# The first two rows of x as two half transfers on two queues, and four stores for six

## The chip, the cores and the metric

The kernel runs on one core of a Trainium2 chip. The metric is the time of one execution on the device in microseconds, and the median of several runs is what is compared. The profile comes from one execution of its own.

## The reference

```python
def reference(x, y):                      # x, y: 8 x 4096 x 512, float32
    gram = np.matmul(x, y.transpose(0, 2, 1))
    diag = np.diagonal(gram, axis1=1, axis2=2)
    diag = diag - diag.max(axis=-1, keepdims=True)
    exp = np.exp(diag)
    return (exp / exp.sum(axis=-1, keepdims=True)).astype(np.float32)
```

Only the diagonal of the product is used. So the work is 8 x 4096 dot products of 512 elements each, and a softmax over the 4096 results of each of the 8 batches. Both inputs have 67 MB, and every byte is read once. The output has 0.13 MB.

## The kernel before

**Tiling.** Four batches form a set, so there are two sets. A set lies on 128 partitions as 4 batches by 32 groups, and each partition holds 128 consecutive rows (of 512 floats) of one batch. A step `t` takes 32 of these rows on each partition: 64 KB of x and 64 KB of y per partition, 8.4 MB each. There are four steps for each set, eight steps in all (`S`). x has two buffers, `xs[0]` and `xs[1]`, used in turn; y has one, `ys`. The tile `side` holds a copy of the last 6 rows of y (`K`), so that the buffer of y comes free sooner.

**The first six steps** (the loop over `range(S - 2)`). `load_x` and `load_y` each issue one transfer of 128 partitions by 64 KB on SyncE's queue. ScalarE copies the last six rows of y to `side`. VectorE multiplies x by y in place: `products` with 26 rows of `ys`, then with the 6 rows of `side` (L78). It then sums 30 of the 32 rows (`sums`, L81), and ScalarE sums the other two (`sums_act`, L86). The order within an engine is written out by hand. SyncE issues its transfers in the program's order, each once its buffer is free and an earlier transfer that used the same completion counter has landed. There are eight such counters, taken in turn.

**The last two steps.** Step 6 loads in one piece and leaves most sums to ScalarE. Step 7 loads x and y in pieces that become smaller towards the end, and VectorE does the dot products row by row (L89) as the pieces land. The last piece is 320 columns of the last row of x (L185).

**The ends.** At the start ScalarE loads the table for the exponential (L124), VectorE and ScalarE each execute an alignment instruction, VectorE writes one constant, and SyncE executes two drains (L130, L131) and then issues the first x. After step 3 the first set's maxima and exponentials are made, and its result `res[0]` is complete in step 4. It is stored only at the end, behind all loads on SyncE's queue, in six pieces of 16, 16, 16, 16, 32 and 32 partitions (L192). The second set's softmax follows the last dot product (`exps`, `normalize`), and ScalarE issues the store of `res[1]` (L194).

Of the kernel before, what the change touches and what calls it, by code (L numbers as in the profile page):

```python
# [11 lines left out]
def kernel(  # L12
# [6 lines left out]
    nc = tc.nc  # L19
# [6 lines left out]
    P = nc.NUM_PARTITIONS  # L26
# [3 lines left out]
    R = 32  # L30
    H = R // 2
# [3 lines left out]
    L = 9  # L35
    E = 64
    V = 5 * D // 8
    U = D - V
    S = B // Q * (C // R)


    xv = x.rearrange("(s b) (j c) d -> s (b j) c d", b=Q, j=G)
# [10 lines left out]
    xs = [t[:, : R * D].rearrange("p (r d) -> p r d", d=D) for t in xflat]  # L53
# [6 lines left out]
    def columns(t, r0, n):  # L60
        c0 = t % (C // R) * R + r0
        return slice(c0, c0 + n)

    def rows(t, r0, n):
        return xs[t % 2][:, r0 : r0 + n, :]

    def dots_of(t, r0, n):
        return diag[t * R // C][:, columns(t, r0, n)]

    def load_x(t, r0, n):  # L70
        nc.sync.dma_start(out=rows(t, r0, n), in_=xv[t * R // C, :, columns(t, r0, n), :])  # L71

    def load_y(t, r0, n):
        nc.sync.dma_start(out=ys[:, r0 : r0 + n, :], in_=yv[t * R // C, :, columns(t, r0, n), :])  # L74

    def products(t, r0, n, yt):
        xt = rows(t, r0, n)
        nc.vector.tensor_tensor(out=xt, in0=xt, in1=yt, op=Alu.mult)  # L78

    def sums(t, r0, n):  # L80
        nc.vector.tensor_reduce(out=dots_of(t, r0, n), in_=rows(t, r0, n), axis=X, op=Alu.add)  # L81

    def sums_act(t, r0, n):
        for r in range(r0, r0 + n):
            row = xs[t % 2][:, r, :]
            nc.scalar.activation(out=row, in_=row, func=Act.Copy, accum_out=dots_of(t, r, 1))  # L86

    def dot(xt, yt, out):
        nc.vector.scalar_tensor_tensor(  # L89
            out=xt, in0=xt, scalar=1.0, in1=yt, op0=Alu.mult, op1=Alu.mult, accum_out=out  # L90
        )

    def dots(t, r0, n):
        for r in range(r0, r0 + n):
            dot(xs[t % 2][:, r, :], ys[:, r, :], dots_of(t, r, 1))
# [12 lines left out]
    def exps(i, d):  # L108
        mxp = small.tile([P, 1], f32, name=f"mxp{i}")
        largest(mxp, d)  # L110
        nmx = over_quadrant(f"nmx{i}", mxp, Alu.max, negate=True)
        sump = small.tile([P, 1], f32, name=f"sump{i}")
        nc.scalar.activation(out=res[i], in_=diag[i][:, :C], func=Act.Exp, bias=nmx, scale=1.0, accum_out=sump)  # L113
        return sump

    def normalize(i, sump):
        total = over_quadrant(f"sum{i}", sump, Alu.add)
        rc = small.tile([P, 1], f32, name=f"rc{i}")
        nc.vector.reciprocal(out=rc, in_=total)  # L119
        nc.vector.tensor_single_scalar(out=res[i], in_=res[i], scalar=rc, op=Alu.mult)  # L120
# [10 lines left out]
    nc.sync.drain()  # L131

    for t in range(S - 2):
        load_x(t, 0, R)
        load_y(t, 0, R)
        nc.scalar.activation(out=side, in_=ys[:, R - K :, :], func=Act.Copy)  # L136
        if t == C // R:
            normalize(0, sump)
        products(t, 0, R - K, ys[:, : R - K, :])
        products(t, R - K, K, side)  # L140
        sums(t, 0, R - W)
        sums_act(t, R - W, W)
        if t == C // R - 1:
            sump = exps(0, diag[0])

    t = S - 2
# [13 lines left out]
    chained = xflat[t % 2][:, R * D : R * D + 1]  # L160
    late = R * D - V
    upto = {load_x: 0, load_y: 0}
# [15 lines left out]
    end = ((t % (C // R)) + 1) * R * D  # L178
    nc.sync.dma_start(out=xt[:, first : late], in_=xrow[:, end - R * D + first : end - V])
    dots(t, done, 1)  # L180
    load_y(t, R - 2, 1)
    dots(t, R - 2, 1)
    load_y(t, R - 1, 1)
    dot(xt[:, late - U : late], yflat[:, late - U : late], chained)
    nc.sync.dma_start(out=xt[:, late : R * D], in_=xrow[:, end - V : end])  # L185
    dot(xt[:, late : R * D + 1], yflat[:, late : R * D + 1], dots_of(t, R - 1, 1))
# [1 line left out]
    met = small.tile([P, C - R], f32, name="met")  # L188
    nc.scalar.activation(out=met, in_=diag[1][:, : C - R], func=Act.Copy)  # L189

    for p, n in ((0, H), (H, H), (2 * H, H), (3 * H, H), (4 * H, 2 * H), (6 * H, 2 * H)):
        nc.sync.dma_start(out=ov[0, p : p + n, :], in_=res[0][p : p + n, :])  # L192
    normalize(1, exps(1, diag[1][:, C - R + H :]))
    nc.scalar.dma_start(out=ov[1], in_=res[1])  # L194
# [30 lines left out]
```

## Time and profile before

| What | us |
|---|---|
| timed runs: median (lowest, highest) | 320.44 (320.05, 320.58), 3 runs |
| profiled execution: span from the first to the last instruction | 318.4 |
| median of the runs less that span | 2.04 |
| VectorE busy | 241.7, in 101 instructions |
| ScalarE busy | 49.8, in 97 instructions |
| DMA, mean over the span | 422 GB/s |

The profile gives the span of its execution but not that execution's whole time, so the runs' median stands beside it. In the parts that follow, "L78" is line 78 of the kernel before. "SPq" and "ACTq" are the queues on which SyncE and ScalarE issue transfers; the time on such a line is that of the issue, not of the transfer. A piece "DMA ys" in the chain is the time from the issue of a load of y to its landing. In a windows line the columns are the window, its length, the busy time of VectorE (DVE), ScalarE (ACT) and GpSimd (POOL) with the number of instructions, the granted clock, the mean busy share of the 16 DMA engines, and GB/s. A DMA packet is counted in the window in which it starts, so in a short window the share can be over 1.

### The profile page before, as it was taken

How to read it: one execution, taken by the hardware profiler on the slowest of the kernel's cores; microseconds unless marked ns; L12 is line 12 of the kernel's file. 1: busy time of each engine (PE TensorE's matmuls, PEld its weight loads, DVE VectorE, ACT ScalarE, POOL GpSimd, SP SyncE). 2: the span in 40 equal slices, each digit the busy share in tenths (PEclk: the TensorE clock that was granted, in tenths of full speed). 3: DMA queues.
4: the chain of work that ended last, by engine and by line, in shares of the span. 5: the costliest groups of instructions: out<-in, count | busy, mean ns of one | idle time of the engine just before them, and what ended most of it. 6: DMA issues, size and time to landing. Idle time of an engine off the chain costs nothing.

```text
span 318.4 us, 320 instructions
## 1 busy us (share of the span) xinstructions
DVE 241.7 (76%) x101; ACT 49.8 (16%) x97; POOL 0.2 (0%) x4
## 2 busy tenths in 40 slices
DVE  0000079994899939999399994999939998499995
ACT  1000030100301003010020102101030100496700
POOL 0000000000000000000000000000000000000000
DMA  9999999999999999999999999999999999999993
GB/s 397 395 395 510 412 395 453 469 395 395 486 436 395 453 469 395 395 486 436 395 395 519 403 395 461 461 395 395 527 395 395 486 436 395 425 415 432 434 410 140
DMA packets 3970, 134.37 MB, mean 422 GB/s; under 512 B 512, under 2 KB 896, under 8 KB 1536
## 3 DMA queue, kind: packets, MB, share of 16 engines
q1 hardware_dynamic: 3824, 134.29, 97.9%
q10 hardware_dynamic: 144, 0.07, 0.1%
q14 instruction: 2, 0.02, 0.0%
HBM read 134.22 MB, written 0.13 MB: 422 GB/s over the span
## 4 chain that ended last, share of the span: by engine, by line
DMA 70%; DVE 28%; issue 0%; SPq 0%; ACT 0%; DVEq 0%
DMA ys<-in_y_dram 59%; DVE xs L78 28%; DMA xs<-in_x_dram 11%; DVE xs L89 0%; SPq L74 0%; SPq L71 0%; DVE res L120 0%; DVE nmx L100 0%; DVE sum L100 0%; ACT res L113 0%; DVE mxp L106 0%; DVE rc L119 0%; DVEq L78 0%; DVEq L89 0%; SPq L131 0%
## 5 line engine op out<-in xcount | busy, mean ns | idle before, releaser
L78 DVE TENSOR_TENSOR xs<-xs,ys 128x13312 f32<-128x13312 f32 (+2 forms) x8 | 96.7, 12091 | 70.3 <-DMA ys<-in_y_dram 70.3
L81 DVE TENSOR_REDUCE diag<-xs 128x30 f32<-128x15360 f32 (+1 forms) x7 | 98.1, 14020 | 0.2
L86 ACT ACTIVATE xs<-xs 128x512 f32<-128x512 f32 x42 | 25.9, 617 | 90.4 <-DVE xs L78 90.4
L136 ACT ACTIVATE side<-ys 128x3072 f32<-128x3072 f32 x6 | 16.6, 2763 | 124.5 <-DMA ys<-in_y_dram 124.5
L89 DVE SCALAR_TENSOR_TENSOR xs<-xs,ys 128x512 f32<-128x512 f32 (+2 forms) x33 | 20.0, 669 | 0.8 <-DMA ys<-in_y_dram 0.7
L78 DVE TENSOR_TENSOR xs<-xs,side 128x3072 f32<-128x3072 f32 x6 | 20.1, 3350 | 0.0
L86 ACT ACTIVATION_READ_ACCUMULATOR xs<-xs 128x1 f32 x42 | 7.8, 187 | 0.0
L150 ACT ACTIVATE xs<-ys 128x4608 f32<-128x4608 f32 x1 | 4.0, 4043 | 19.9 <-DMA ys<-in_y_dram 19.9
L113 ACT ACTIVATE res<-diag,nmx 128x128 f32<-128x128 f32 x2 | 0.8, 401 | 29.8 <-DVE nmx L100 29.8
L78 DVE TENSOR_TENSOR xs<-xs,xs 128x4608 f32<-128x4608 f32 x1 | 5.0, 4951 | 0.0
L89 DVE DVE_READ_ACCUMULATOR xs<-xs,ys 128x1 f32 x33 | 2.7, 81 | 0.0
L124 ACT ACT_TABLE_LOAD x1 | 1.3, 1283 | 0.7 <-PEq L209 0.7
L100 DVE TRANSPOSE_TENSOR_REDUCE sum<-sump 128x1 f32<-128x32 f32 x2 | 0.4, 212 | 1.2 <-ACT res L113 1.2
L128 DVE MEMSET ys<- 128x1 f32 x1 | 0.1, 59 | 1.4 <-PEq L209 1.4
L120 DVE TENSOR_SCALAR res<-res,rc 128x128 f32<-128x128 f32 x2 | 0.6, 286 | 0.1
L106 DVE TENSOR_REDUCE mxp<-diag 128x1 f32<-128x128 f32 (+1 forms) x2 | 0.5, 228 | 0.1
L100 DVE TRANSPOSE_TENSOR_REDUCE nmx<-mxp 128x1 f32<-128x32 f32 x2 | 0.4, 212 | 0.1
L106 DVE TENSOR_REDUCE diag<-diag 128x1 f32<-128x64 f32 (+1 forms) x2 | 0.4, 202 | 0.0
L119 DVE RECIPROCAL rc<-sum 128x1 f32<-128x1 f32 x2 | 0.3, 164 | 0.1
L113 ACT ACTIVATION_READ_ACCUMULATOR res<-diag,nmx 128x1 f32 x2 | 0.4, 186 | 0.0
L189 ACT ACTIVATE met<-diag 128x96 f32<-128x96 f32 x1 | 0.3, 282 | 0.0
L209 POOL MEMSET const-bfloat16-1.0<- 128x1 bf16 x1 | 0.1, 101 | 0.0
(3 smaller groups left out, 0.3 us busy)
## 6 DMA issues: line engine op xcount, KB each, us to landing
ys<-in_y_dram SPq DMA_DIRECT2D x1, 4352.0 KB, 14.8
xs<-in_x_dram SPq DMA_DIRECT2D x1, 3840.0 KB, 14.1
ys<-in_y_dram SPq DMA_DIRECT2D x1, 2304.0 KB, 12.2
xs<-in_x_dram SPq DMA_DIRECT2D x1, 2048.0 KB, 19.3
xs<-in_x_dram SPq DMA_DIRECT2D x1, 1536.0 KB, 15.5
ys<-in_y_dram SPq DMA_DIRECT2D x1, 768.0 KB, 16.9
ys<-in_y_dram SPq DMA_DIRECT2D x3, 256.0 KB, 18.2
xs<-in_x_dram SPq DMA_DIRECT2D x1, 608.0 KB, 18.0
```

The lines of the kernel that those rows point to most:

```text
L78: nc.vector.tensor_tensor(out=xt, in0=xt, in1=yt, op=Alu.mult)
L81: nc.vector.tensor_reduce(out=dots_of(t, r0, n), in_=rows(t, r0, n), axis=X, op=Alu.add)
L86: nc.scalar.activation(out=row, in_=row, func=Act.Copy, accum_out=dots_of(t, r, 1))
L89: nc.vector.scalar_tensor_tensor(out=xt, in0=xt, scalar=1.0, in1=yt, op0=Alu.mult, op1=Alu.mult, accum_out=out)
L100: nc.vector.tensor_reduce(out=got, in_=column.to_broadcast([P, G]), axis=X, op=op, negate=negate, apply_transpose=True)
L106: nc.vector.tensor_reduce(out=out, in_=d, axis=X, op=Alu.max)
L113: nc.scalar.activation(out=res[i], in_=diag[i][:, :C], func=Act.Exp, bias=nmx, scale=1.0, accum_out=sump)
L119: nc.vector.reciprocal(out=rc, in_=total)
L120: nc.vector.tensor_single_scalar(out=res[i], in_=res[i], scalar=rc, op=Alu.mult)
L124: nc.scalar.preload_act_table(Act.Exp)
L136: nc.scalar.activation(out=side, in_=ys[:, R - K :, :], func=Act.Copy)
L150: nc.scalar.activation(out=spare, in_=ys[:, F - L : F, :], func=Act.Copy)
```

## The change

In step 0 the first two rows of x (4 KB on each partition) come in two transfers of their own: partitions 64 to 127 on SyncE's queue and partitions 0 to 63 on ScalarE's. The other 30 rows follow on SyncE's queue as one transfer of 128 partitions by 60 KB. All other loads are as before. On ScalarE the new issue stands behind the table load and the alignment instruction, and ahead of the first copy to `side`. At the end `res[0]` is stored in four pieces of 32 partitions instead of six. There are as many transfers in all as before, 32: two more at the start and two fewer at the end. VectorE's first product, ScalarE's and SyncE's later uses of this x buffer wait for the pieces of it.

```diff
+    A = 2
...
     for t in range(S - 2):
-        load_x(t, 0, R)
+        if t:
+            load_x(t, 0, R)
+        else:
+            low, up = slice(0, P // 2), slice(P // 2, P)
+            for engine, half in ((nc.sync, up), (nc.scalar, low)):
+                engine.dma_start(out=xs[0][half, :A, :], in_=xv[0, half, :A, :])
+            load_x(0, A, R - A)
         load_y(t, 0, R)
...
-    for p, n in ((0, H), (H, H), (2 * H, H), (3 * H, H), (4 * H, 2 * H), (6 * H, 2 * H)):
+    for p, n in ((0, 2 * H), (2 * H, 2 * H), (4 * H, 2 * H), (6 * H, 2 * H)):
         nc.sync.dma_start(out=ov[0, p : p + n, :], in_=res[0][p : p + n, :])
```

## The prediction

> **What bounds the kernel now.** I read the chain that ended last on the profile's page first, then the same chain in order of time, then the rates by window. The page:
>
> ```profile
> span 318.4 us, 320 instructions
> DMA  9999999999999999999999999999999999999993
> q14 instruction: 2, 0.02, 0.0%
> HBM read 134.22 MB, written 0.13 MB: 422 GB/s over the span
> DMA 70%; DVE 28%; issue 0%; SPq 0%; ACT 0%; DVEq 0%
> ```
>
> The DMA engines are busy in all slices but the last. The chain calls 28% VectorE, but in order of time it shows what these pieces are (start, length, what):
>
> ```profile
> 0.83 0.39 SPq L71
> 1.22 0.06 issue
> 1.27 40.69 DMA ys<-in_y_dram
> ...
> 42.06 14.04 DVE xs L78
> 56.10 0.02 SPq L74
> 56.12 0.05 issue
> 56.17 24.62 DMA ys<-in_y_dram
> ...
> 298.78 0.02 issue
> 298.80 14.80 DMA xs<-in_x_dram
> 313.60 0.03 issue
> ```
>
> SyncE issues the next y when VectorE has left the y buffer (56.17), and y then lands 24.62 us later. That looks like a wait on VectorE, but the next x is in the queue meanwhile. For the stretch up to 60 us, the instructions on the x tiles end with the times from issue to landing of the first two x loads:
>
> ```profile
> L71 SPq DMA_DIRECT2D xs<-in_x_dram x2: 390/660/929, 0.8 to 1.7; - x2
> DMA to landing us min/median/max: 21.8/40.7/59.6
> ```
>
> The second x, issued at 1.74 (timeline row below), lands at 1.74 + 59.6 = 61.3. The y behind it was issued at 56.17, so the queue holds work for 5.2 us more than it needs. VectorE is hidden by that margin. What is left is one stream of bytes through 16 DMA engines. The windows (us, then DVE, ACT and POOL busy, clock, DMA share, GB/s) give its rate, its start and its end; a row counts in the window in which it starts:
>
> ```profile
> 1.80:1.85 0.05, 0.00 (x0) 0.05 (x1) 0.00 (x0) 1.00 0.91 164
> 1.85:2.00 0.15, 0.00 (x0) 0.15 (x1) 0.00 (x0) 1.00 10.31 3550
> 2.00:2.40 0.40, 0.00 (x0) 0.00 (x1) 0.00 (x0) 1.00 1.38 492
> 2.40:2.80 0.40, 0.00 (x0) 0.00 (x0) 0.00 (x0) 1.00 1.20 492
> 2.80:3.00 0.20, 0.00 (x0) 0.00 (x0) 0.00 (x0) 1.00 1.55 655
> 3.00:4.00 1.00, 0.00 (x0) 0.00 (x0) 0.00 (x0) 1.00 0.00 0
> 120.00:200.00 80.00, 70.26 (x12) 10.95 (x13) 0.00 (x0) 1.00 1.00 433
> 312.00:312.50 0.50, 0.50 (x1) 0.00 (x0) 0.00 (x0) 1.00 1.03 390
> 312.50:313.00 0.50, 0.50 (x3) 0.00 (x0) 0.00 (x0) 1.00 0.96 322
> 313.00:313.20 0.20, 0.20 (x2) 0.00 (x0) 0.00 (x0) 1.00 0.48 132
> 313.20:313.60 0.40, 0.37 (x4) 0.00 (x0) 0.00 (x0) 1.00 0.24 59
> ```
>
> At 433 GB/s the 134.22 MB take 310.0 us, and between SyncE's first issue (0.83) and the last landing (313.60) lie 312.8. So 2.8 us at most are lost, nearly all at the two ends. The first windows show how. A row of x is 32 x 2 KB = 65.5 KB for each partition. In 1.85 to 2.00 there start 3550 x 0.15 = 532 KB, which is 8 rows and one 8 KB packet of the instruction queue (its two packets are 0.02 MB together, and the other starts just before, 164 x 0.05 = 8 KB). Then 492 x 0.40 = 197 KB, 3 rows; again 3; and 655 x 0.20 = 131 KB, 2 rows. That makes 16: one first row for each engine. The first eight engines start before 2.00, the last two after 2.80. No engine starts a second row before 4.00. Every engine has the same bytes to move, so an engine that starts late ends late, and the last landing waits for the latest: after 313.00 the share falls to 0.48 and 0.24, some engines are done and others aren't.
>
> **The change part by part.**
>
> *Two small transfers first.* SyncE's first issue now has 64 rows of 4 KB, not 128 of 65.5 KB, and ScalarE issues the other 64. The bytes are the same. What can change is the lag of the last engine. Today it is at least 2.80 - 2.00 = 0.80 us and at most 3.00 - 1.85 = 1.15; I take the middle, 0.98. No load in the trace has 64 partitions or short rows and idle engines. The nearest thing is the last store, 128 rows of 512 B, which ScalarE issues when nothing else moves:
>
> ```profile
> 315.98 0.37 ACTq L194 DMA_DIRECT2D out_dram<-res  x1
> ```
>
> and in the windows
>
> ```profile
> 316.00:316.80 0.80, 0.00 (x0) 0.00 (x0) 0.00 (x0) 1.00 0.00 0
> 316.80:317.00 0.20, 0.00 (x0) 0.00 (x0) 0.00 (x0) 1.00 0.53 166
> 317.00:317.20 0.20, 0.00 (x0) 0.00 (x0) 0.00 (x0) 1.00 0.55 162
> 317.20:318.00 0.80, 0.00 (x0) 0.00 (x0) 0.00 (x0) 1.00 0.00 0
> ```
>
> All its rows, 166 x 0.20 + 162 x 0.20 = 65.6 KB, start within 0.40 us. An engine has 8 of them, so the engines' first rows lie within about 0.20 of each other. If 4 KB rows are dealt out like that, the lag falls from 0.98 to 0.20: a gain of 0.78, between 0.60 and, with no lag left, 1.15. The other end is no gain, since a store isn't a load (rival 1). I take 0.78, by the nearest row.
>
> *More rows.* Each engine gets 8 more rows (8 of 4 KB in front of 8 that are shorter by as much) and two completion marks more at the start. A 512 B row takes 0.53 x 0.20 x 16 / 65 = 26 ns; at 433 / 16 = 27.1 GB/s its bytes take 19 ns, so a row costs 7 ns beside its bytes. Ten times 7 ns is 0.07 us on the stream, a loss.
>
> *One issue more on SyncE ahead of the first y and the second x.* The timeline has today's issues:
>
> ```profile
> 0.72 1.28 ACT L124 ACT_TABLE_LOAD   x1 [0.72 <-PEq L209]
> 0.83 0.39 SPq L71 DMA_DIRECT2D xs<-in_x_dram  x1
> 1.27 0.42 SPq L74 DMA_DIRECT2D ys<-in_y_dram  x1
> 1.74 0.93 SPq L71 DMA_DIRECT2D xs<-in_x_dram  x1
> ```
>
> One issue is 1.27 - 0.83 = 0.44 us. The rest of the first x goes out at 1.27, the first y at about 1.71, the second x at about 2.18. The last two hide behind the first x, which lands only at 0.83 + 21.8 = 22.6. The rest of x hides behind the small rows: 8 x 4 KB at 27.1 GB/s keep an engine busy for 1.2 us. If that cover were gone (no ScalarE rows yet, so only 0.6 us of work), an engine would stand still for up to 0.4 us.
>
> *ScalarE's issue.* It stands behind the table load in ScalarE's program, with the first copy of y into the side tile queued behind it; that copy waits for y until 42 us, so it doesn't notice. If ScalarE's issue goes out while the table load runs, at about 0.8, nothing is late. If it waits, it goes out at 0.72 + 1.28 = 2.00 (rival 2).
>
> *More completions to wait for.* VectorE's first product waits for four loads, and SyncE's third x for three completions of the first x where it had one. A wait costs about 0.05 (the issue pieces of the chain), covered by the 5.2 us margin; if that were gone, 0.1.
>
> *Four stores for six.* Before, in SyncE's timeline:
>
> ```profile
> 304.24 8.57 SPq L192 DMA_DIRECT2D out_dram<-res  x6
> ```
>
> The last piece of x was issued at 298.80, ahead of all stores, so no load stands behind a store in the queue. Two issues less are free for SyncE, and the same 128 rows are written. Nothing waits for them but the end at 318.4, long after. Zero, and nothing either way while the last store (315.98) ends the run.
>
> **Sum.** Span 318.4 - 0.78 + 0.07 = 317.7. The profile gives the span of its execution and not its whole time; the median of the timed runs is 320.44, so 2.04 lie around the span, and the change touches none of it: 317.7 + 2.04 = 319.7 us. With the bounds of the lag (gain 0.60 to 1.15) this case reaches from 319.36 to 319.91. A measurement of this kernel tells about 0.2%, that is 0.64 us, from no change; the limits are 319.80 and 321.08.
>
> **The rivals.**
>
> *1. The lag stays.* The small rows are no better than the long ones: the late engines are late for the first read itself, or for the two instruction packets that start just ahead of the rows or among them, not for the way in which the rows are dealt out. For it: eight engines did start together within 0.15 us with long rows, so dealing alone doesn't explain the rest. Against it: the store's even start. Price: from a partial gain of half, 0.39 - 0.07 = 0.32, to a loss of 0.07, so 320.1 to 320.5, say 320.3: no change. The Trainium skill, page "DMA: Bandwidth & Descriptors", section "Rules for kernel authors", speaks against this change: of two transfers to disjoint partition halves it says "Don't bother", since both halves go over the same 16 engines and issuing from two engines saves issue time alone. By that rule the time would be this rival's; no run here shows it yet.
>
> *2. ScalarE's half is late, and 64 rows don't feed all engines well.* Its issue waits for the table load until 2.00, and by the store's rows (issue 315.98, first row after 316.80) its rows start some 0.82 to 1.02 later, at about 2.9. If SyncE's 64 rows meanwhile occupy only half of the engines, the others begin with the rest of x, which is issued 0.44 later than today's first x, with today's lag: +0.44. If the half transfers also run at half the rate, 4 rows an engine take 1.2 instead of 0.6 us: +0.61 more, +1.05 in all. It decides from the point where ScalarE's issue starts later than SyncE's second, at 1.27. For it: the order of ScalarE's program, and that no load in the trace covers half the partitions. Against it: the rest of x fills every engine soon after. I take +0.8, 321.2 us, between 320.9 and 321.5.
>
> **How the numbers follow.** The forecast, 319.7, has 0.50: the trace has a lag of 0.8 us or more that the last landing pays in full, and the one row that is near says that short rows start evenly. Rival 1 has 0.25, rival 2 has 0.25. Of the forecast's own range, 319.36 to 319.91, a fifth lies over 319.80, of which I take 0.06 out of its 0.50: faster 0.44. Rival 2 lies nearly all over 321.08 but for its lower end: slower 0.22. The rest, 0.06 + 0.25 + 0.03, is within 0.2%: 0.34. The range begins at 319.3, under the forecast's best case, takes in rival 1 whole, and ends at 321.3, past the middle of rival 2; it leaves out some 0.1 of that rival and less below. Cases of both signs hold most of the chance; the likeliest one's own range is the one just named.
>
> **What would show it.** Right: in windows of 0.1 us the 4 KB rows of both queues start together near 1.85; the last piece of x lands at about 312.9, not 313.60; after SyncE's first issue the rest of x follows at 1.27; the tail from that landing to the end stays 4.8 us (318.4 - 313.60). Rival 1: the last landing stays at 313.5 or later with ScalarE's issue before 1.27. Rival 2: ScalarE's issue at or after 2.00, and windows between 2 and 4 us with engines that start nothing. The prediction is wrong altogether if the steady rate leaves 433 GB/s, or if a wait in the middle of the chain has lost its 5.2 us of cover.

## The result and the profile after

| | before | after |
|---|---|---|
| timed side by side, median (lowest, highest) | 320.09 (319.95, 320.58), 5 runs | 321.11 (320.69, 321.61), 5 runs |
| span of the profiled execution | 318.4 | 319.4 |

The medians differ by 1.02 us, a loss; the ratio of the runs is 1.0036, with an interval of 1.0025 to 1.0047. The forecast was a gain of 0.7. The time lies in the predicted range, but on the other side of no change. Of all the timed executions below, one (346.37 us in middle16) was far slower than the others of its kernel, and it is left out of that run's ratio.

The page of after, in the rows that answer to those of before:

```profile
span 319.4 us, 322 instructions
DMA  7999999999999999999999999999999999999993
HBM read 134.22 MB, written 0.13 MB: 421 GB/s over the span
DMA 70%; DVE 28%; SPq 1%; issue 0%; ACT 0%; DVEq 0%
```

The bytes and the shape of the chain are the same. What differs is the first slice of the DMA row, which falls from 9 to 7. The chain of after, in order of time (start, length, what):

```profile
2.05 41.89 DMA ys<-in_y_dram
43.94 0.03 issue
...
135.32 24.43 DMA ys<-in_y_dram
...
173.94 24.45 DMA ys<-in_y_dram
...
299.90 14.80 DMA xs<-in_x_dram
314.70 0.03 issue
```

The first y has landed at 43.94. Before, it was 1.27 + 40.69 = 41.96, so 1.98 us are lost by then. The last piece of x lands at 314.70, against 313.60: 1.10 late. The tail behind it is 319.4 - 314.70 = 4.7 (4.8 before). So everything is lost within the first 44 us, and 0.88 of it is won back on the way; to that I return below.

The timeline of the start of after:

```profile
0.72 1.28 ACT L125 ACT_TABLE_LOAD   x1 [0.72 <-PEq L216]
0.83 0.54 SPq L140 DMA_DIRECT2D xs<-in_x_dram  x1
1.21 2.38 ACTq L140 DMA_DIRECT2D xs<-in_x_dram  x1
1.43 0.57 SPq L72 DMA_DIRECT2D xs<-in_x_dram  x1
2.05 0.74 SPq L75 DMA_DIRECT2D ys<-in_y_dram  x1
2.83 0.63 SPq L72 DMA_DIRECT2D xs<-in_x_dram  x1
```

ScalarE's issue did not wait for the end of the table load (2.00). It began at 1.21, but it took 2.38 us. SyncE's 64 rows took 0.54 to issue, where 128 rows of 64 KB had taken 0.39. And the DMA issues of after (KB, us from issue to landing) show how late ScalarE's half is:

```profile
xs<-in_x_dram SPq DMA_DIRECT2D x1, 256.0 KB, 4.0
xs<-in_x_dram ACTq DMA_DIRECT2D x1, 256.0 KB, 18.9
```

The windows of after (columns as in the prediction):

```profile
1.80:2.10 0.30, 0.00 (x0) 0.20 (x1) 0.00 (x0) 1.00 0.06 27
2.10:2.20 0.10, 0.00 (x0) 0.00 (x0) 0.00 (x0) 1.00 1.40 287
...
8.00:18.88 10.88, 0.00 (x0) 0.00 (x0) 0.00 (x0) 1.00 1.00 386
```

Up to 2.10 there starts nothing but one packet of the instruction queue (27 x 0.30 = 8 KB). The first rows of data start after 2.10, in the trace at 2.16; before, it was 1.85. Then SyncE's 4 KB rows run, then two 60 KB rows on each engine, and only at 8.0 do ScalarE's rows begin, in turn with the 60 KB rows. Four turns (one row of 60 KB and one of 4 KB on each engine, 16 x 4 x 65.5 KB = 4.19 MB) take 10.88 us at 386 GB/s, while all 16 engines are busy (share 1.00). At the steady 433 GB/s these bytes take 9.68. In the trace it is not ScalarE's rows that are slow: they take 0.17 us in the mean, and the 60 KB rows between them 2.55, where such a row takes 2.27 when it runs beside nothing but full-width rows (scalar128 below).

### The profile page after: what moved, and what is told of

Its sections match the earlier page's. It is cut to its first block, busy times and chain, and to the rows that moved or that the text cites. A ratio compares the mean times of both kernels' runs of the same rounds, so it can differ in the third digit from the quotient of the medians.

```text
span 319.4 us, 322 instructions
## 1 busy us (share of the span) xinstructions
DVE 241.7 (76%) x101; ACT 49.8 (16%) x97; POOL 0.2 (0%) x4
## 4 chain that ended last, share of the span: by engine, by line
DMA 70%; DVE 28%; SPq 1%; issue 0%; ACT 0%; DVEq 0%
DMA ys<-in_y_dram 59%; DVE xs L79 28%; DMA xs<-in_x_dram 11%; SPq L72 0%; SPq L140 0%; DVE xs L90 0%; SPq L75 0%; DVE res L121 0%; DVE sum L101 0%; DVE nmx L101 0%; ACT res L114 0%; DVE mxp L107 0%; DVEq L79 0%; DVE rc L120 0%; DVEq L90 0%
## 5 line engine op out<-in xcount | busy, mean ns | idle before, releaser
L79 DVE TENSOR_TENSOR xs<-xs,side 128x3072 f32<-128x3072 f32 x6 | 20.1, 3350 | 0.0
```

## The experiments

The expectations set two theories against each other. Theory 1 says that the mixing of two queues costs the time: rows of ScalarE's queue among SyncE's. Theory 2 says that a transfer that covers 64 partitions is slow in itself, whoever issues it; for the runs in step 2 it is narrowed to a loss at the start alone. Later it is put more sharply, as theory P: which partitions a transfer writes sets its rate. All edits are to the kernel after, but for stores4, which is the kernel before with the four stores. Each ratio is to the kernel before on the same chip. Landings are compared with those of the first profile of before.

### The parts of the change

**stores4** has the four stores alone, and loads x as before.

> The kernel before with the four stores alone. Both theories, that the loss comes from ScalarE's rows breaking into SyncE's stream and that it comes from transfers of 64 partitions: no change, 320.1 us within 0.3, first y landed at about 41.96 us. If the stores cost something, some of the +1.0 us shows here, in the stretch behind the last landing.

Measured: 319.88 against 319.82, 1.0005 [0.9996, 1.0013]. The chain of stores4 has its first y at 42.08:

```profile
1.27 40.81 DMA ys<-in_y_dram
```

The stores are free. **one128** keeps the two rows ahead, as one transfer of 128 partitions on SyncE:

```diff
-            for engine, half in ((nc.sync, up), (nc.scalar, low)):
-                engine.dma_start(out=xs[0][half, :A, :], in_=xv[0, half, :A, :])
+            load_x(0, 0, A)
```

> The first two rows as one transfer of 128 partitions on SyncE's queue, the rest as in the changed kernel. Theory 1: as with both halves on SyncE's queue within 0.3 us. Theory 2: clearly faster than that one, by 0.5 us or more, back at 320.1. If short rows at the start do what the prediction said, the last engine's lag falls and the last landing comes before 313.6.

Measured: 319.83, 1.0001 [0.9992, 1.0010]. The windows and the chain of one128:

```profile
1.80:2.10 0.30, 0.00 (x0) 0.21 (x1) 0.00 (x0) 1.00 1.34 205
```

```profile
1.75 40.58 DMA ys<-in_y_dram
```

205 x 0.30 = 62 KB start early, as before the change. With one issue more ahead of it, the first y lands at 42.33, 0.37 later than before, and nothing of that is seen in the time. Short rows first neither gain nor lose: the gain that I had forecast for them isn't there. The trace shows why: the 60 KB rows of the 16 engines, behind eight short rows each, begin between 3.63 and 4.49. That is a spread of 0.86 us, inside the 0.80 to 1.15 that the prediction read for the long rows of before, so the lag was not dealt away. **both_sync** keeps the halves and takes away the second queue:

```diff
-            for engine, half in ((nc.sync, up), (nc.scalar, low)):
+            for engine, half in ((nc.sync, up), (nc.sync, low)):
```

> The changed kernel with both half transfers on SyncE's queue. Theory 1 (each 4 KB row of ScalarE's queue that comes between two 60 KB rows of SyncE's costs an engine about 0.3 us, four of them 1.2 us, and two issues at once delay the first rows by 0.3): both losses go, first y landed at 42.0 to 42.6 us instead of 43.94, total 319.3 to 320.4. Theory 2 (64 partitions feed the engines badly, on whatever queue): most of the loss stays, first y at 43 or later, total 321 or more.

Measured: 322.10, 1.0064 [1.0049, 1.0078]. The windows, the timeline and the chain of both_sync:

```profile
1.80:2.10 0.30, 0.00 (x0) 0.21 (x1) 0.00 (x0) 1.00 0.21 55
2.00:6.00 4.00, 0.00 (x0) 0.01 (x1) 0.00 (x0) 1.00 1.11 362
```

```profile
0.84 1.19 SPq L140 DMA_DIRECT2D xs<-in_x_dram  x2
2.07 0.59 SPq L72 DMA_DIRECT2D xs<-in_x_dram  x1
```

```profile
2.70 42.04 DMA ys<-in_y_dram
```

On one queue the loss is about twice as large (ratios 1.0064 and 1.0036). The first y lands at 44.74, about 2.7 late. Theory 1 can't explain that. **scalar16** leaves ScalarE 16 partitions, and SyncE 112:

```diff
-            low, up = slice(0, P // 2), slice(P // 2, P)
+            low, up = slice(0, P // 8), slice(P // 8, P)
```

> ScalarE issues 16 partitions of the first two rows (one row an engine instead of four), SyncE the other 112. Theory 1: one break of 0.3 us instead of four, so about 0.9 us less than the changed kernel: first y landed at 43.0 instead of 43.94, total about 320.2. Theory 2: two uneven parts feed the engines better than halves too, but no step of 0.3 for each row of ScalarE's is seen: the loss goes as a whole or stays as a whole.

Measured: 320.84, 1.0027 [1.0016, 1.0038]. The first y in the chain of scalar16 lands at 43.90:

```profile
1.74 42.16 DMA ys<-in_y_dram
```

With an eighth of the partitions on ScalarE instead of half, the loss is nearly that of the change (ratios 1.0027 and 1.0036). It does not shrink with the number of rows on the second queue. What a cut into 112 and 16 partitions costs by itself isn't shown: no run loads such parts with long rows.

### The same pieces with a full queue

The start mixes several things: late first rows, longer issues, idle engines. So the halves were moved to step 2, where the queue is full:

```diff
-        if t:
+        if t != 2:
...
-                engine.dma_start(out=xs[0][half, :A, :], in_=xv[0, half, :A, :])
-            load_x(0, A, R - A)
+                engine.dma_start(out=xs[0][half, :A, :], in_=xv[0, half, columns(2, 0, A), :])
+            load_x(2, A, R - A)
```

**middle** has the split of the change there, **middle16** that of scalar16, **middle_sync** that of both_sync.

> The half transfers moved from step 0 to step 2, where the queue is full: 64 partitions on SyncE's queue, 64 on ScalarE's. Theory 1 (two queues in one stream cost time on every engine): the 4 ScalarE rows of each engine break into the stream near 100 us and cost 0.3 us each, the y of step 2 lands 1.2 to 1.6 us later than with both halves on SyncE, total 321.0 to 321.4. Theory 2 (the loss is at the start alone, half transfers that begin late and leave engines without work): no change, 319.8 to 320.0.

> The same in step 2 with 16 partitions (one row an engine) on ScalarE's queue and 112 on SyncE's. Theory 1: one break, 0.3 us if the price is by row, 0.6 to 1.0 if it is by transfer, total 320.2 to 320.8. Theory 2: no change, 319.8 to 320.0.

> The same in step 2 with both half transfers on SyncE's queue. Both theories: no change, 319.8 to 320.0, since the queue is full when they are issued. If this one is slower too, a transfer of 64 partitions costs the engines time in any place.

Measured: middle 322.49, 1.0088 [1.0076, 1.0101]; middle16 321.15, 1.0042 [1.0029, 1.0055]; middle_sync 321.72, 1.0060 [1.0048, 1.0072]. There is a loss in all three. Theory 1 had expected less in the two with ScalarE (321.0 to 321.4 and 320.2 to 320.8) and none in middle_sync; theory 2, as it was narrowed, had expected none at all. The y of step 2, in the chains of before, of middle and of middle_sync:

```profile
94.98 24.44 DMA ys<-in_y_dram
```

```profile
96.06 26.00 DMA ys<-in_y_dram
```

```profile
96.22 25.48 DMA ys<-in_y_dram
```

They land at 119.42, 122.06 and 121.70. So the loss doesn't need an empty queue, nor a late first row, nor ScalarE: cutting the partitions costs time with a full queue too. In the trace of middle_sync the 128 half rows of 4 KB take 0.30 us in the mean, about twice the 0.16 of such a row of a full-width transfer (scalar128 below). That is 1.1 us for the eight rows of an engine, and 2.3 are lost. The rest stands on long rows: the first 16 rows of 60 KB behind the halves take 3.23 in the mean, those that follow 2.27. Why these are slow isn't shown. **whole_halves** enlarges the suspect: the whole x of step 0 as two transfers of 64 partitions on SyncE.

```diff
-            for engine, half in ((nc.sync, up), (nc.scalar, low)):
-                engine.dma_start(out=xs[0][half, :A, :], in_=xv[0, half, :A, :])
-            load_x(0, A, R - A)
+            for half in (up, low):
+                nc.sync.dma_start(out=xs[0][half, :R, :], in_=xv[0, half, :R, :])
```

> In step 0 x comes as two transfers of 64 partitions and all 32 rows, on SyncE's queue: the halves without short rows and without ScalarE. Theory 2: the first rows start about 0.3 us later than with 128 partitions (2.15 instead of 1.85), and the time is 0.3 us more, 320.1 to 320.2; if the engines are left without work between the two, more, up to 322. Theory 1 alone: no change, 319.8 to 320.0.

Measured: 341.07, 1.0666 [1.0653, 1.0680], 21.4 us more. No expectation came near it. The windows of whole_halves:

```profile
1.80:2.10 0.30, 0.00 (x0) 0.21 (x1) 0.00 (x0) 1.00 0.10 27
2.10:2.20 0.10, 0.00 (x0) 0.00 (x0) 0.00 (x0) 1.00 14.52 3277
10.00:20.00 10.00, 0.00 (x0) 0.00 (x0) 0.00 (x0) 1.00 1.02 210
...
50.00:60.00 10.00, 0.00 (x0) 0.00 (x0) 0.00 (x0) 1.00 0.97 419
```

The row of 10 to 20 us decides. All 16 engines are busy (1.02), and they move 210 GB/s, not 433: a 64 KB row takes 5.13 us in the trace, not 2.42. At 210 GB/s the 8.39 MB take 39.9 us, at 433 they take 19.4; the difference is 20.6. The start adds 0.3, since the first rows come in 2.10 to 2.20 here too (1.85 in before); about 0.5 of the 21.4 is left over. The share of busy time alone would not have shown it: an engine that writes at half its rate is as busy as any.

**across** asks whether it is the number of partitions or which ones. SyncE loads the same x in three transfers: the middle 64 partitions, then the first 32, then the last 32. The new lines stand in place of the loop over the halves and of the load behind it.

```diff
+            for half in (slice(P // 4, 3 * P // 4), slice(0, P // 4), slice(3 * P // 4, P)):
+                nc.sync.dma_start(out=xs[0][half, :R, :], in_=xv[0, half, :R, :])
```

> The first x as three transfers on SyncE's queue with all 32 rows: partitions 32 to 95, then 0 to 31, then 96 to 127. Theory P (what counts is which part of SBUF a transfer writes: 0 to 63 are one half of the ways in, 64 to 127 the other, and 32 to 95 reach both): the first 4.2 MB move at the full 433 GB/s with rows of about 2.42 us, the other two parts at 210 GB/s, and the time is 10 to 11 us over the kernel before, half of what two halves cost. Theory N (the number of partitions counts): 64 partitions run at 210 GB/s wherever they lie and 32 not faster, 21 us or more.

Measured: 330.75, 1.0339 [1.0323, 1.0356], 10.9 more. The windows of across, the first inside the middle 64 partitions, the second inside the outer ones:

```profile
5.10:12.35 7.25, 0.00 (x0) 0.00 (x0) 0.00 (x0) 1.00 1.01 434
16.85:26.85 10.00, 0.00 (x0) 0.00 (x0) 0.00 (x0) 1.00 1.01 210
```

64 partitions that lie across the middle run at the full rate, and 32 on one side at half of it. So it isn't the number. The Trainium skill, page "SBUF — State Buffer", section "Door 1: The DMA port swizzle (why `[64,N]` ≈ `[32,N]`)", gives a reason: partitions 0 to 63 share 8 of the 16 ports through which transfers write the memory, 64 to 127 the other 8, and a step of 32 stays on the same port. Its 8 ports come to some 218 GB/s; here it was 210. Its map also gives all 16 ports to partitions 32 to 95, which agrees with 434. The runs themselves show that the choice of partitions sets the rate. Each partition also reads its own part of x, and no run gives the same partitions other addresses; that the limit is on the writing side rests on that page.

### The second queue by itself

**scalar128** has the two first rows of all 128 partitions on ScalarE's queue; **rows_two** splits by row and not by partition, row 1 on SyncE and row 0 on ScalarE. In both, the new lines stand in place of the loop over the halves.

```diff
+            nc.scalar.dma_start(out=xs[0][:, :A, :], in_=xv[0, :, :A, :])
```

```diff
+            for engine, r in ((nc.sync, 1), (nc.scalar, 0)):
+                engine.dma_start(out=xs[0][:, r : r + 1, :], in_=xv[0, :, r : r + 1, :])
```

> In step 0 the first two rows of all 128 partitions go on ScalarE's queue (8 rows an engine), the other 30 rows on SyncE's. Theory P: rows from two queues cost nothing when together they reach all of SBUF; first y landed at 42.0 to 42.6 us, total 319.6 to 320.2. Theory 1 (queue mixing costs 0.3 us a row): 8 x 0.3 = 2.4 us more, 322.

> As the changed kernel, but the first two rows are split by row and not by partition: row 1 of all 128 partitions on SyncE's queue, row 0 on ScalarE's. Theory P: the loss of the changed kernel is gone, 319.6 to 320.3, first rows at 1.85 us and not 2.16. Theory 1: as slow as the changed kernel or slower, 321 or more.

Measured: scalar128 319.72 against 319.86, 0.9994 [0.9985, 1.0003]; rows_two 319.93, 1.0000 [0.9991, 1.0009]. The windows of scalar128, four turns of one 60 KB row and one row of ScalarE's, and those of rows_two at the start:

```profile
9.30:18.98 9.68, 0.00 (x0) 0.00 (x0) 0.00 (x0) 1.00 1.00 433
```

```profile
1.80:2.10 0.30, 0.00 (x0) 0.21 (x1) 0.00 (x0) 1.00 0.75 82
```

ScalarE issues as slowly here, and its rows take turns with SyncE's as in the change. At full width the four turns take 9.68 us, not 10.88, and every 60 KB row in them takes 2.27 in the trace. In rows_two the first rows start at 1.86, as in before (1.85). Mixing the queues is free. What the change loses comes from the cut between partitions alone: cut by row, the same bytes on the same two queues are level with before.

**middle128** puts two rows of all 128 partitions on ScalarE's queue in step 2, and the other 30 on SyncE's.

> In step 2 the first two rows of all 128 partitions go on ScalarE's queue, the rest on SyncE's. Theory P: no change, 319.6 to 320.1, the y of step 2 lands at about 119.5 us. Theory 1: 8 x 0.3 = 2.4 us more, landed at 121.8, total 322.

Measured: 322.61, 1.0082 [1.0068, 1.0097], where theory P had expected no change. Theory 1's number, 322, comes near, but not by its mechanism: the y of step 2 has landed when ScalarE's copy of it starts at 119.63, as theory P said (119.5, theory 1 121.8), and in the trace ScalarE's rows take 0.16 us and the 64 KB rows among them 2.42, as alone. So this is another loss. The chain and the timeline of middle128:

```profile
98.30 23.84 DMA xs<-in_x_dram
```

```profile
122.22 14.02 DVE L79 TENSOR_TENSOR xs<-xs,ys 128x13312 f32<-128x13312 f32 x1 [7.78 <-DMA xs<-in_x_dram]
155.78 0.33 SPq L72 DMA_DIRECT2D xs<-in_x_dram  x1
```

ScalarE's rows get one turn for each row of SyncE's, so the x of step 2 is complete only at 122.14, behind its own y. VectorE starts late, the x of step 4 is issued late, at 155.78, and that was too late: its rows start between 157.3 and 160.4, and the engines run empty meanwhile. The 5.2 us of cover that the prediction counted are not all usable: an issue some 2 us before the queue runs dry already costs time. In middle a part of the loss may be of this kind; middle_sync, with no ScalarE, is the clean one.

### Both halves at the same time

If the two halves ran side by side, their parts of the memory would both be in use. **scalar_first** issues ScalarE's half ahead of the table load; **scalar_first128** does so with both rows of all 128 partitions.

```diff
+    nc.scalar.dma_start(out=xs[0][: P // 2, :A, :], in_=xv[0, : P // 2, :A, :])
     nc.scalar.preload_act_table(Act.Exp)
...
-            for engine, half in ((nc.sync, up), (nc.scalar, low)):
-                engine.dma_start(out=xs[0][half, :A, :], in_=xv[0, half, :A, :])
+            nc.sync.dma_start(out=xs[0][up, :A, :], in_=xv[0, up, :A, :])
```

> The changed kernel with ScalarE's half issued ahead of its table load, at about 0.7 us, before SyncE's half at 0.83. If only halves that move alone lose (theory P), both halves now move together and reach all of SBUF: first y landed at 42.3 to 42.7 us (0.3 late at the start is left) instead of 43.94, total 319.7 to 320.4. If a half loses its time even beside the other one, total 321 or more, as changed.

> ScalarE issues the first two rows of all 128 partitions ahead of its table load, SyncE the other 30 rows. By the prediction's reason (short rows start evenly, so the last engine's lag falls): first y landed at 41.3 or earlier, total 319.3 or less. By the runs so far (the lag of 0.6 to 0.7 us comes back with any start): 319.6 to 320.1, no change.

Measured: scalar_first 321.35 (320.31 to 321.88), 1.0045 [1.0029, 1.0061]; scalar_first128 319.71, 0.9997 [0.9989, 1.0006]. The timeline of scalar_first, and its first y in the chain:

```profile
0.73 0.58 ACTq L125 DMA_DIRECT2D xs<-in_x_dram  x1
0.84 0.55 SPq L140 DMA_DIRECT2D xs<-in_x_dram  x1
```

```profile
2.25 40.81 DMA ys<-in_y_dram
```

The issues are 0.11 apart, yet in the trace ScalarE's rows start from 2.09 to 3.54 and SyncE's only from 2.90 to 4.58, so they overlap in part. The first y lands at 43.06, still 1 us late. This profile is of an execution of 320.43; four of the seven took 321.35 or more, and no trace shows those. So this attempt did not bring the halves together, and whether halves that truly run side by side are free stays open. scalar_first128 says that an earlier start by ScalarE gains nothing.

**before_again** and **after_again** are one more profile of each kernel, on the chip of scalar_first.

> The kernel before once more, for its profile. If the slower stretches between 40 and 200 us belong to its start, from the first y's landing to the last x's landing it takes again 271.2 to 271.7 us. If they are chance, it may take 270.8 as the changed kernel did.

> The changed kernel once more, for its profile. If its even stretch belongs to its start, it takes again 270.7 to 270.9 us from the first y's landing to the last x's landing. If chance, 271.2 to 271.7. The first y lands at about 43.9 us in either case.

Their spans are 318.3 and 318.6. The first y in the chain of before_again, then in that of after_again, and the four turns with ScalarE's rows in the windows of after_again:

```profile
1.28 40.72 DMA ys<-in_y_dram
```

```profile
2.05 41.11 DMA ys<-in_y_dram
```

```profile
7.96:18.30 10.34, 0.00 (x0) 0.00 (x0) 0.00 (x0) 1.00 1.02 405
```

The landings are 42.01 and 43.17. So the loss at the first y is 1.2 in one execution and 2.0 in another, and the four turns cost 10.34 - 9.68 = 0.66 here and 1.20 there. At half rate a 4 KB row of 0.15 us takes 0.15 more, 0.6 for four: the size of after_again fits that, and the first profile has as much again. But in neither does that time stand on the half rows, which take 0.17: it stands on the 60 KB rows between them, 2.46 us in the mean here and 2.55 there, for 2.27. So the half rate that whole_halves shows doesn't explain this part as it stands; how a half row slows a long row beside it stays open.

## Why the prediction was wrong

**The step that failed** is the first term of the sum: "If 4 KB rows are dealt out like that, the lag falls from 0.98 to 0.20: a gain of 0.78". The term was priced by the only short rows in the trace, a store of 128 partitions, and the transfers of the change have 64; the sum went on to price their rows at the full 27.1 GB/s of an engine. So there are two errors.

- *The gain does not exist.* The lag was not due to the long rows. one128 and rows_two start with short rows, scalar128 and scalar_first128 take two rows a partition off SyncE's first transfer, and all four are within 0.1% of before. In one128 the engines are still spread over 0.86 us behind their short rows. That is rival 1's case, the lag that stays; which of the reasons it named is the true one isn't shown.
- *The halves cost time.* By whole_halves' 210 GB/s a half of 262 KB takes 1.25 us in place of 0.61, the rows beside and behind the halves are slowed too, and the first row comes 0.31 later (2.16 for 1.85). For the first profile that gives, as an estimate, up to 0.64 for SyncE's half, 1.20 measured for ScalarE's four turns and 0.31 for the start, 2.15 at most; 1.98 was lost at the first y.

Since one stream bounds the kernel, what is lost there reaches the end, less what the stream wins back on the way. In after, 314.70 - 43.94 = 270.76 us lie between the first y and the last x; before, 313.60 - 41.96 = 271.64. Two rows of the chain of before, to be held against 24.43 and 24.45 of after:

```profile
133.60 24.78 DMA ys<-in_y_dram
...
172.56 24.65 DMA ys<-in_y_dram
```

The same happened in the second profiles (271.57 before, about 270.75 after), so it is probably no chance. But it isn't tied to the loss: stores4, with the loads of before, took 271.27, and scalar128, whose first y landed at 42.25, 270.88. Why some starts make the later stream more even stays open.

**Rival 2** had the right size: 321.2, with a term "if the half transfers also run at half the rate". That clause names the half rate that whole_halves shows, and it deserved to stand as a case of its own. Its condition was wrong. ScalarE issued at 1.21 and not after 2.00, and a transfer of 64 partitions occupies all 16 engines, not half of them (a busy share of 1.02 in whole_halves). By the signs that the prediction named, the profile was rival 1's: ScalarE's issue before 1.27 and the last landing, 314.70, after 313.5. So it is in part luck that the time lies in the range: the range was widened upwards for a case that did not come about as it was told. ScalarE's rows are late for another reason: by the time its issue of 2.38 us was out, each engine had two 60 KB rows ahead of them.

**The rule that I weighed**, "Don't bother" from the Trainium skill's page "DMA: Bandwidth & Descriptors", section "Rules for kernel authors", had the right advice. It says that the halves share the engines, and from that I concluded that the time would not change. The price is higher: each half is also slow by itself. The Trainium skill's page "SBUF — State Buffer", in the section cited above, gives the half rate, and I had not drawn on it.

**Right:** the stores cost nothing (stores4). SyncE's additional issue is hidden (one128). Eight more short rows an engine cost too little to be seen. The tail stayed at 4.7. No wait of steps 1 to 7 lost its cover, as the stretch from first y to last x became shorter, not longer. 2.04 around the span was 0.2 too much: the executions with both numbers, such as 321.24 - 319.4 and 320.13 - 318.3, give 1.8.

## What to carry to other kernels

Split a transfer along its rows, not between partitions 0 to 63 and 64 to 127, unless each half is too small to matter: the rate depends on which partitions a transfer covers, and a busy share of 1.0 hides it. Price a new transfer by a row of the same partitions, and where the trace has none, give the half-rate case a chance of its own. A small transfer on a second queue is free in bandwidth but lands late, since its rows take turns with long ones; put there only what isn't needed soon.

## What the runs showed of the hardware beyond that

- ScalarE's issue, right behind SyncE's, took 2.38 us in after, 2.42 in scalar128 and 2.58 in scalar16; ahead of the table load it took 0.58. What it waited for isn't shown.
- As an engine's first issue, a transfer of one half of the partitions took 0.54 us (after) to 0.58 (scalar_first, on ScalarE), one of 128 partitions 0.39 (before). SyncE's first row came 0.3 later.
- Two queues take turns row by row, whatever their length: in scalar128, from 9.30 to 18.98, 64 rows of 60 KB and 64 of 4 KB start.
- The landing of a transfer on the second queue came about one long row after its last row had ended: at 20.1 after 17.30 in after, at 122.14 after 119.38 in middle128.
- An issue about 2 us before the queue ran dry still left engines idle (middle128: issued at 155.78, the last rows ended by 158.02, the last engine began again at 160.43).
